# Activation blocks of a Strassen-Winograd down projection: summed by spreading and adding DMAs in DRAM instead of by GpSimd in SBUF

## The chip, the cores and the metric

The kernel runs on one NeuronCore of a Trainium2 chip. TensorE (PE) multiplies into PSUM; PEld is its weight load. VectorE (DVE) and ScalarE (ACT) do the elementwise work, GpSimd (POOL) does a little of it and issues its own DMAs, and SyncE (SP) issues the other DMAs. Each engine takes its instructions in order, and semaphores tie the engines together. The metric is the device time of one execution in microseconds (us), the median over repeated runs.

## The reference

One decoder layer on x of 1024 positions by 1024 channels, float32: RMSNorm, a joint input projection for a retention group (4 heads) and a gated spatial group (4 groups), an output projection with a residual, then the part that matters here, and a last RMSNorm:

```python
h = rmsnorm(x, ffn_norm_g[l])
up = causal_depthwise_conv(h @ w_up[l], conv_w[l], conv_b[l])   # width 3
a, bgate = jnp.split(up, [D_FF], axis=-1)                       # D_FF = 2816
x = x + (jax.nn.silu(a) * bgate) @ w_down[l]
```

## The kernel before, in words

Channels lie on the 128 partitions and positions on the free axis, so 2816 channels are 22 tiles of 128 x 1024. All matmuls work on float32 split into a high and a low part (`split_w`, L113 and L114: a ScalarE copy `h` and a VectorE difference `l`), and each of the three big projections is cut into 2 x 2 blocks and done with seven block products instead of eight.

**Up projection and gate.** `unit` (u3 to u21) makes the two 128 x 1024 rows `ra` and `rb` of one channel tile: PE sums products in PSUM banks (X, Y, Z, L147), ScalarE and VectorE take them out (L205, L221, L228, L247, L160), and both prepare the next unit's weights. `conv` (L791, L800, L803) then works on a finished pair: ScalarE scales `ra` into a tile `cv` (L788), VectorE adds two shifted taps (L791), ScalarE applies silu (L800), and `gate` multiplies by the other branch (L803). Tiles `cv`, `ra` and `rb`, and many others, are drawn from one ring of 38 buffers (`up`); a new tile's first writer waits until the last reader of the old one is through.

**Activation blocks.** Tiles 2j and 2j+1 (called `e` and `o`, pair j, 11 pairs) are the upper and lower row block of the down projection's activation, and the halves 0 and 1 of the positions are its column blocks. `blocks_of` (L814 to L822) makes the seven blocks that the seven products need and stores them in the DRAM tile `gb`, in four DMAs from GpSimd's queue; four of the blocks are differences, made by four GpSimd subtractions per pair (L820) in place.

**Down projection.** The seven products run in the order `SEQ` = 2, 1, 5, 6, 3, 7, 4. `load_act` (L851) fetches a product's blocks, two pairs at a time, and splits them (L852, L853); product 2's fetches (g20 to g24) go through GpSimd's queue, the rest through SP's. `load_wt` (L868) fetches the weights. `down` (L893) multiplies and `acc` (L898) adds a PSUM result to the residual rows `x2`. For the last pair, products 2 and 1 take their block from SBUF directly.

PE's order is written out by hand from u20 on; everything else, on every engine, is ordered by a planner that simulates the program. Names in traces drop their numbers: `cv` is any gate tile, `gb` the DRAM blocks.

Of the kernel before, what the change touches and what calls it, by code (L numbers as in the profile page):

```python
# [10 lines left out]
F32 = mybir.dt.float32  # L11
F32R = mybir.dt.float32r
AF = mybir.ActivationFunctionType
ALU = mybir.AluOpType

P = 128
# [8 lines left out]
HALF = 512  # L25
# [40 lines left out]
def decoder_layer(ctx, tc, io, out):  # L66
    nc = tc.nc
# [8 lines left out]
    def U(name, dt=F32, shape=(P, 1024)):  # L76
        return up.tile(list(shape), dt, tag="u", name=name)
# [4 lines left out]
    def A(name):  # L82
        return pp.tile([P, HALF], F32, tag="acc", name=name, bufs=5)

    def M(name, shape=(P, 512)):
        return pp.tile(list(shape), F32, tag="sm", name=name, bufs=3)
# [16 lines left out]
    hs = lambda t, h: t[:, h * HALF:(h + 1) * HALF]  # L103
# [18 lines left out]
    def split(src, name):  # L122
        h, l = U(name + "h", F32R, src.shape), U(name + "l", F32R, src.shape)
        nc.scalar.activation(h, src, AF.Copy)
        nc.vector.tensor_tensor(l, src, h.bitcast(F32), ALU.subtract)
        return h, l
# [25 lines left out]
    class Unit:  # L152
# [9 lines left out]
        def prep(u, src, key, eng=None):  # L162
            h, l = split_w(src, u.name + key, eng=eng)
            return [(h[:, o:o + u.kh], l[:, o:o + u.kh]) for o in range(0, src.shape[1], u.kh)]
# [293 lines left out]
    for half in range(2):  # L458
        ps = M(f"r1bc{half}")
# [14 lines left out]
    def small4(name, f, n=4):  # L474
        ps = M(name, (P, 4, P))
        for j in range(n):
            f(ps[:, j], j)
        return ps
# [15 lines left out]
    for h in range(NH):  # L494
# [10 lines left out]
        for half in range(2):  # L505
            ps = small4(f"pS{h}{half}", lambda o, j: nc.tensor.matmul(o, kT[:, cut(half * 4 + j)], qT[:, cut(half * 4 + j)], start=True, stop=True))
# [189 lines left out]
    for u in us:  # L696
        h, l = split(u.wa, u.name + "a")
# [77 lines left out]

    BLK = {k: i for i, k in enumerate(("R11", "R21", "R22", "T1", "T3", "T4", "T2"))}
    gbs = [dp.tile([P, 7, n, HALF], F32, name=f"gb{n}") for n in (KH - 1, 1)]
    halves = lambda t: t.rearrange("p (a b) -> p a b", b=HALF)  # L780

# [17 lines left out]
    def silu(t):  # L799
        nc.scalar.activation(t, t, AF.Silu)  # L800

    def gate(i, a, b, eng=None):
        (eng or nc.vector).tensor_tensor(a, a, b, ALU.mult)  # L803
        g[i] = halves(a)

    g = {}
# [1 line left out]
    def conv(ra, rb, i):  # L808
        a = Taps(ra, i).all()
        silu(a)  # L810
        gate(i, a, Taps(rb, FT + i).all())


    def blocks_of(j):  # L814
        e, o = g.pop(2 * j), g.pop(2 * j + 1)
        gb, j = gbs[j // (KH - 1)], j % (KH - 1)
        nc.gpsimd.dma_start(gb[:, 0, j], e[:, 0])  # L817
        nc.gpsimd.dma_start(gb[:, 1:3, j], o)  # L818
        for x, y, z in ((e[:, 0], e[:, 1], e[:, 0]), (e[:, 1], o[:, 1], e[:, 1]), (o[:, 1], o[:, 1], e[:, 0]), (o[:, 0], o[:, 0], o[:, 1])):
            nc.gpsimd.tensor_tensor(x, y, z, ALU.subtract)  # L820
        nc.gpsimd.dma_start(gb[:, 3:5, j], e)
        nc.gpsimd.dma_start(gb[:, 5:7, j], o)  # L822

    class Up(Unit):
        def __init__(u, i):
# [16 lines left out]
    def load_act(i, j):  # L842
        n = min(2, KH - 2 * j)
        src = gbs[0][:, BLK[KEY[i]], 2 * j:2 * j + 2] if n == 2 else gbs[1][:, BLK[KEY[i]]]
        if n == 2:
            h, l = [U(f"g{i}{j}{x}", F32R, PAIR) for x in "hl"]
        else:
            e = U(f"g{i}{j}e", F32R, PAIR)
            h, l = e[:, :1], e[:, 1:]
        x = l.bitcast(F32)  # L850
        (nc.gpsimd if i == SEQ[0] else nc.sync).dma_start(x, src)  # L851
        nc.scalar.activation(h, x, AF.Copy)  # L852
        nc.vector.tensor_tensor(l, x, h.bitcast(F32), ALU.subtract)  # L853
        act[i] += [(h[:, m], l[:, m]) for m in range(n)]

    def last_act(i, x):
# [27 lines left out]
    def load_x2(n):  # L884
        x2[n] = U(f"x2{n}")
        nc.sync.dma_start(x2[n], x2d[:, n])

    def down(ps, i, p, start, ks, stop, cols=slice(0, HALF)):
        first = start
        todo = [(k, s) for k in ks for s in range(2)] + [(k, 2) for k in ks]  # L890
        for n, (k, s) in enumerate(todo):
            w, r = wts[i][p * KH + k], act[i][k]
            nc.tensor.matmul(ps, w[s // 2], r[s % 2][:, cols], start=first, stop=stop and n == len(todo) - 1, skip_group_check=True)  # L893
            first = False

    def acc(n, half, ps):
        o = hs(x2[n], half)
        nc.vector.tensor_tensor(o, ps, o, ALU.add)  # L898

    PREP = {2: [(load_act, j) for j in range(5)]}  # L900
    for i in SEQ[1:]:
        PREP[i] = [(f, int(j)) for f, j in zip([load_act, load_act, load_wt] * 3 + [load_wt] * 3, "010231452345")]
        if i == 1:
            PREP[i] = [(load_act, j) for j in range(5)] + [(load_wt, j) for j in range(6)]
# [10 lines left out]
    def conv_next():  # L915
        nonlocal done
        conv(*todo[done], done)
        if done % 2:
            blocks_of(done // 2)
        done += 1  # L920
# [36 lines left out]
    e, o = g[FT - 2], g[FT - 1]  # L957
    last_act(2, o[:, 0])
    last1 = U("g1e", F32R, PAIR)
    nc.scalar.activation(last1[:, 0], e[:, 0], AF.Copy)  # L960
    nc.vector.tensor_tensor(last1[:, 1], e[:, 0], last1[:, 0].bitcast(F32), ALU.subtract)
    blocks_of(KH - 1)


# [24 lines left out]
    Z = [M(f"dZ{p}") for p in range(3)] + [A("dZ3")]  # L989
# [3 lines left out]
    for p in range(4):  # L993
        down(Z[p], 2, p, False, [KH - 1], True)
        if p:
            load_x2(2 * p + 2) if p < 3 else None
        acc(2 * p, 0, Z[p])
    prep(1, 20)
    act[1].append((last1[:, 0], last1[:, 1]))
    for i, nxt in zip(SEQ[1:-1], SEQ[2:]):  # L1000
        for p in range(4):
            prep(nxt, 3)
            if i in (1, 6, 7):
                if i == 1:
                    X[p] = A(f"dX{p}")
                ps = X[p]
            else:
                if i == 5:
                    load_x2(2 * p + 1)
                ps = M(f"dY{i}{p}")  # L1010
            down(ps, i, p, i in (1, 5, 3), range(KH), True)
            for n, half in {1: [(0, 0)], 5: [(0, 1), (1, 1)], 6: [(0, 1)], 3: [(0, 1)], 7: [(1, 1)]}[i]:
                acc(2 * p + n, half, ps)
            if i == 7:
                for b in (ba, bb, bc):
                    b.square(2 * p)
    manual.close()

    with tc.manual_schedule(engines={mybir.EngineType.PE, mybir.EngineType.DVE, mybir.EngineType.Activation}):
# [8 lines left out]
        for k in range(8):  # L1028
            s, p = divmod(k, 4)
            b = (bb, bc)[s]  # L1030
            ps = X[p][:, b.blk]
            down(ps, 4, p, False, range(KH), True, b.blk)
            y = x2[2 * p + 1][:, b.blk]
# [51 lines left out]
```

## Time and profile before

| | us |
|---|---|
| median of 3 runs | 1063.68 |
| lowest, highest | 1059.34, 1066.58 |
| profiled execution, its own time | 1061.0 |
| its span | 1059.2 |
| PE busy in the span | 1023.9 (97%) |
| DVE busy | 823.0 (78%) |
| ACT busy | 486.6 (46%) |
| POOL busy | 173.3 (16%) |
| mean granted TensorE clock | 0.993 of full |

Times in the trace are microseconds from the span's start. The up projection with its gates fills about 440 to 833, the down projection 833 to the end. A row of a group of instructions gives line, engine, operation, output and inputs, shapes and count, then busy time, mean duration in ns, and the idle time of that engine just before, with what ended it. A row of the timeline gives start, duration, engine, line, what was done, and in brackets the idle time before it and its releaser.

### The profile page before, as it was taken

The numbers are of one execution on the slowest core, as the hardware profiler recorded it, in microseconds if no ns is written. First come the engines' busy times: TensorE is split into PE (matmuls) and PEld (weight loads), VectorE is DVE, ScalarE is ACT, GpSimd is POOL, SyncE is SP. The second block draws the span as 40 slices with busy tenths as digits, with TensorE's granted clock in tenths as the row PEclk, the third lists the DMA queues.
The fourth block names the chain that finished last, engine by engine and source line by source line (L and its number), as shares of the span: only waits on it lengthen the run. The fifth ranks groups of instructions, "written<-read, shape, count | busy, mean of one in ns | idle before, by whom it ended". The sixth has DMA issues, their size and how long they took to land.

```text
span 1059.2 us, 12678 instructions
## 1 busy us (share of the span) xinstructions
PE 1023.9 (97%) x4794; PEld 846.7 (80%) x4794; DVE 823.0 (78%) x1022; ACT 486.6 (46%) x684; POOL 173.3 (16%) x132
## 2 busy tenths in 40 slices
PE   7899999999999999999999999999999999999996
PEld 5677888888888888788888778778888888878896
DVE  6958886968968378856789998987869877886565
ACT  6563444334364253535445535444535643344440
POOL 0002330411310000000214152323034120000000
PEclk9989999999999999999999999999999999999998
DMA  8151031121356240011323233332244788974514
GB/s 301 68 199 40 23 110 63 49 81 62 99 197 222 100 159 20 21 60 58 113 90 114 106 129 129 110 119 99 82 149 132 263 308 295 372 242 151 203 51 159
DMA packets 48445, 141.57 MB, mean 134 GB/s; under 512 B 5056, under 2 KB 9536, under 8 KB 48384
## 3 DMA queue, kind: packets, MB, share of 16 engines
q1 hardware_dynamic: 42032, 117.96, 32.3%
q0 software_dynamic: 6352, 22.81, 5.7%
q8 instruction: 37, 0.61, 0.2%
q14 instruction: 24, 0.20, 0.1%
HBM read 109.03 MB, written 31.72 MB: 133 GB/s over the span
## 4 chain that ended last, share of the span: by engine, by line
PE 72%; DVE 17%; issue 5%; ACT 4%; DMA 1%; POOL 1%; SPq 0%; DVEq 0%; ACTq 0%; POOLq 0%
PE dX L893 11%; PE po L135 8%; PE dY L893 6%; DVE cv L791 3%; PE dZ L893 3%; PE G3X L147 1%; PE G1X L147 1%; PE A3X L147 1%; PE B3X L147 1%; PE u2X L147 1%; PE u21X L147 1%; PE u20X L147 1%; PE u18X L147 1%; PE u3X L147 1%; PE A0X L147 1%
## 5 line engine op out<-in xcount | busy, mean ns | idle before, releaser
L817 POOL DMA_DIRECT2D gb<-cv x11 | 6.5, 588 | 265.3 <-DVE cv L803 254.3
L800 ACT ACTIVATE cv<-cv 128x1024 f32<-128x1024 f32 x22 | 23.3, 1059 | 47.7 <-DVE cv L791 47.7
L820 POOL TENSOR_TENSOR cv<-cv 128x512 f32<-128x512 f32 x22 | 40.1, 1825 | 26.3 <-DMA gb<-cv 14.9
L820 POOL TENSOR_TENSOR cv<-cv,cv 128x512 f32<-128x512 f32 x22 | 36.4, 1656 | 4.9 <-DMA gb<-cv 2.8
L818 POOL DMA_DIRECT2D gb<-cv x11 | 7.8, 710 | 127.7 <-DVE cv L803 127.7
L803 DVE TENSOR_TENSOR cv<-cv,cv 128x1024 f32<-128x1024 f32 x22 | 26.8, 1218 | 0.0
L650 DVE TENSOR_TENSOR xr<-po,xr 128x512 f32<-128x512 f32 x16 | 10.8, 688 | 19.9 <-PE po L135 19.9
L973 ACT ACTIVATE x3q<-x 128x256 f32<-128x256 f32 (+1 forms) x21 | 9.3, 483 | 33.1 <-DVE x L1034 28.2
L656 ACT ACTIVATE xq<-xr 128x512 f32<-128x512 f32 x14 | 8.8, 628 | 24.1 <-DVE xr L650 17.0
L541 ACT ACTIVATE sT<-po 128x128 f32<-128x128 f32 x32 | 8.4, 277 | 13.3 <-PE po L533 13.2
L878 DVE TENSOR_TENSOR wd<-wd,wd 128x1024 f32<-128x1024 f32 (+1 forms) x6 | 6.8, 1135 | 9.4 <-DMA wd<-in_w_down 9.4
L975 DVE TENSOR_TENSOR sq<-sq,x3q 128x256 f32<-128x256 f32 (+1 forms) x20 | 9.8, 516 | 4.2 <-ACT x3q L973 3.8
L984 DVE SCALAR_TENSOR_TENSOR x<-x,vec,r 128x256 f32<-128x256 f32 (+1 forms) x24 | 12.0, 566 | 0.8 <-PE r L617 0.8
L660 DVE TENSOR_TENSOR sq<-sq,xq 128x512 f32<-128x512 f32 x13 | 8.9, 688 | 3.2 <-ACT xq L656 3.0
L875 DVE TENSOR_TENSOR ds<-wd,wd 128x1024 f32<-128x1024 f32 (+1 forms) x6 | 6.8, 1134 | 5.8 <-DMA wd<-in_w_down 5.8
L341 DVE SCALAR_TENSOR_TENSOR x<-x,vec,x 128x512 f32<-128x512 f32 x16 | 11.0, 747 | 0.0
L670 ACT ACTIVATE nx<-xr,vec 128x512 f32<-128x512 f32 x16 | 10.8, 708 | 0.0
L504 ACT ACTIVATE kn<-pk,vec 128x512 f32<-128x512 f32 x8 | 5.2, 680 | 11.8 <-PE pk L503 11.8
L360 ACT ACTIVATE xn<-xn 128x1024 f32<-128x1024 f32 x8 | 8.4, 1053 | 3.4 <-DMA xn<-in_xN 3.2
L673 DVE TENSOR_TENSOR nx<-nx,r 128x1024 f32<-128x1024 f32 x8 | 9.5, 1216 | 0.4 <-PE r L617 0.4
L1034 DVE TENSOR_TENSOR x<-dX,x 128x256 f32<-128x256 f32 x8 | 3.4, 424 | 8.0 <-PE dX L893 8.0
L898 DVE TENSOR_TENSOR x<-dY,x 128x512 f32<-128x512 f32 x12 | 8.1, 685 | 1.4 <-DMA x<-x2d 1.4
(5664 smaller groups left out, 3795.7 us busy)
## 6 DMA issues: line engine op xcount, KB each, us to landing
wd<-in_w_down SPq DMA_DIRECT2D x45, 512.0 KB, 4.4
gb<-cv POOLq DMA_DIRECT2D x33, 512.0 KB, 3.3
wo<-in_w_out SPq DMA_DIRECT2D x10, 512.0 KB, 3.7
x<-in_xT SPq DMA_DIRECT2D x8, 512.0 KB, 9.2
xn<-in_xN SPq DMA_DIRECT2D x8, 512.0 KB, 6.7
xr<-in_xT SPq DMA_DIRECT2D x8, 512.0 KB, 6.0
x2d<-xr SPq DMA_DIRECT2D x8, 512.0 KB, 3.1
x<-x2d SPq DMA_DIRECT2D x8, 512.0 KB, 7.2
```

The lines of the kernel that those rows point to most:

```text
L135: nc.tensor.matmul(ps, a, b, start=(k == 0 and t == 0), stop=(k == n - 1 and t == 2))
L147: nc.tensor.matmul(ps, a[:, k], b, start=(start and i == 0), stop=(i == 3 * n - 1), skip_group_check=not start)
L341: nc.vector.scalar_tensor_tensor(o[:, m], x[:, m], V("g1", 2 * j + m), y[:, m], ALU.mult, op)
L650: nc.vector.tensor_tensor(u.y, u.ps, u.y, ALU.add)
L670: nc.scalar.activation(nx[n // 2][:, n % 2], xr[th][n // 2][:, n % 2], AF.Identity, scale=V("g2", n))
L791: nc.vector.scalar_tensor_tensor(u.t[:, d:], u.r[:, :S - d], V("cw", 88 - 44 * d + u.i), u.t[:, d:], ALU.mult, ALU.add)
L800: nc.scalar.activation(t, t, AF.Silu)
L803: (eng or nc.vector).tensor_tensor(a, a, b, ALU.mult)
L820: nc.gpsimd.tensor_tensor(x, y, z, ALU.subtract)
L893: nc.tensor.matmul(ps, w[s // 2], r[s % 2][:, cols], start=first, stop=stop and n == len(todo) - 1, skip_group_check=True)
L975: nc.vector.tensor_tensor(sq[:, u.blk], sq[:, u.blk], u.t, ALU.add)
L984: nc.vector.scalar_tensor_tensor(y, y, V("gf", n), u.nr.rs, ALU.mult, ALU.mult)
```

## The change

`blocks_of` no longer subtracts. `gate` multiplies each half of the positions by itself, and one of the halves (half 1 of an even tile, half 0 of an odd one) comes out negated, by a scalar_tensor_tensor with -1. With the signs set, every block is a sum of halves, and the blocks are laid out in `gb` so that each half goes to neighbouring ones: three DMAs per pair write a half into 4, 2 and 1 blocks at once (one source, repeated), then three DMAs with `accum_op=add` add a half to 4, 2 and 1 blocks that are already there. The three adding DMAs of a pair overlap one another's blocks, so each waits for the one before. Products 2 and 5 get negated blocks, and `acc` subtracts their results; product 4's block is negated back while it is split.

```diff
-    BLK = {k: i for i, k in enumerate(("R11", "R21", "R22", "T1", "T3", "T4", "T2"))}
+    BLK = {k: i for i, k in enumerate(("R11", "T1", "T4", "T2", "T3", "R22", "R21"))}
...
-    def gate(i, a, b, eng=None):
-        (eng or nc.vector).tensor_tensor(a, a, b, ALU.mult)
+    def gate(i, a, b):
+        neg = 1 - i % 2
+        for k in range(2):
+            o, x = hs(a, k), hs(b, k)
+            if k == neg:
+                nc.vector.scalar_tensor_tensor(o, o, -1.0, x, ALU.mult, ALU.mult)
+            else:
+                nc.vector.tensor_tensor(o, o, x, ALU.mult)
         g[i] = halves(a)
...
     def blocks_of(j):
         e, o = g.pop(2 * j), g.pop(2 * j + 1)
         gb, j = gbs[j // (KH - 1)], j % (KH - 1)
-        nc.gpsimd.dma_start(gb[:, 0, j], e[:, 0])
-        nc.gpsimd.dma_start(gb[:, 1:3, j], o)
-        for x, y, z in ((e[:, 0], e[:, 1], e[:, 0]), (e[:, 1], o[:, 1], e[:, 1]), (o[:, 1], o[:, 1], e[:, 0]), (o[:, 0], o[:, 0], o[:, 1])):
-            nc.gpsimd.tensor_tensor(x, y, z, ALU.subtract)
-        nc.gpsimd.dma_start(gb[:, 3:5, j], e)
-        nc.gpsimd.dma_start(gb[:, 5:7, j], o)
+        def put(blk, x, **kw):
+            n = blk[1] - blk[0]
+            nc.gpsimd.dma_start(gb[:, blk[0]:blk[1], j], x.unsqueeze(1).to_broadcast([P, n, HALF]), **kw)
+
+        put((0, 4), e[:, 0])
+        put((4, 6), o[:, 1])
+        put((6, 7), o[:, 0])
+        put((1, 5), e[:, 1], accum_op=ALU.add)
+        put((2, 4), o[:, 1], accum_op=ALU.add)
+        put((2, 3), o[:, 0], accum_op=ALU.add)
...
-        nc.scalar.activation(h, x, AF.Copy)
-        nc.vector.tensor_tensor(l, x, h.bitcast(F32), ALU.subtract)
+        if i == 4:
+            nc.scalar.activation(h, x, AF.Copy, scale=-1.0)
+            nc.vector.scalar_tensor_tensor(l, x, -1.0, h.bitcast(F32), ALU.mult, ALU.subtract)
+        else:
+            nc.scalar.activation(h, x, AF.Copy)
+            nc.vector.tensor_tensor(l, x, h.bitcast(F32), ALU.subtract)
...
-    def acc(n, half, ps):
+    def acc(n, half, ps, op=ALU.add):
         o = hs(x2[n], half)
-        nc.vector.tensor_tensor(o, ps, o, ALU.add)
+        nc.vector.tensor_tensor(o, o, ps, op)
...
-        acc(2 * p, 0, Z[p])
+        acc(2 * p, 0, Z[p], ALU.subtract)
...
-                acc(2 * p + n, half, ps)
+                acc(2 * p + n, half, ps, ALU.subtract if i == 5 else ALU.add)
```

The planner's order moves with it. On GpSimd's queue, pair 0 (its tiles are cv_3739 for `e`, cv_3874 or cv_3875 for `o`) stands before so, the waits in brackets (DMASW is a semaphore of GpSimd's DMAs):

```order
L817 DMA gb_3525<-cv_3739 128x512 [waits DVE_49]
L820 TENSOR_TENSOR cv_3739<-cv_3739 128x512 [waits DMASW0_49,DMAHW7_49,PE_49,Activation_49]
L818 DMA gb_3525<-cv_3874 128x2x512 [waits DVE_49]
L820 TENSOR_TENSOR cv_3739<-cv_3874,cv_3739 128x512 [waits Pool_49]
L821 DMA gb_3525<-cv_3739 128x2x512 [waits Pool_49]
L820 TENSOR_TENSOR cv_3874<-cv_3874,cv_3739 128x512 [waits DMAHW1_49,DMASW1_49,DMAHW2_49,PE_49,Activation_49]
L820 TENSOR_TENSOR cv_3874<-cv_3874 128x512 [waits Pool_49]
L822 DMA gb_3525<-cv_3874 128x2x512 [waits Pool_49]
```

and in the changed kernel so, with the three plain DMAs first and the three adding ones behind them:

```order
L827 DMA gb_3525<-cv_3739 128x4x512 [waits DVE_49,Activation_49]
L827 DMA gb_3525<-cv_3875 128x512 [waits DVE_49,Activation_49]
L827 DMA gb_3525<-cv_3875 128x2x512 [waits DVE_49]
L827 DMA gb_3525<-cv_3739 128x4x512 [waits DMASW2_49,DMASW0_49]
L827 DMA gb_3525<-cv_3875 128x2x512 [waits DMASW3_49]
L827 DMA gb_3525<-cv_3875 128x512 [waits DMASW4_49]
```

The four subtractions are gone; the last three DMAs each wait for DMAs of the same pair to land.

On ACT, the buffer of pair 1's `e` goes to another tile. Before, the first `cv` of u5 waited for DVE and ACT alone:

```order
L205 ACTIVATE u8p_4344<-u8X 128x512 [waits PE_49]
L113 ACTIVATE u8ch<-u8t 128x1024 [waits PE_49]
L788 ACTIVATE cv_4305<-u5ra,vec 128x1024 [waits DVE_49,Activation_49]
L788 ACTIVATE cv_4310<-u5rb,vec 128x1024 [waits DVE_49]
L113 ACTIVATE u8dh<-u8w_4324 128x512 [waits DMAHW7_49,PE_49,Activation_49]
L221 ACTIVATE u8p_4381<-u8Y 128x512 [waits PE_49]
```

and in the changed kernel:

```order
L205 ACTIVATE u8p_4344<-u8X 128x512 [waits PE_49]
L789 ACTIVATE cv_4306<-u5ra,vec 128x1024 [waits DMASW6_49,DMASW1_49]
L789 ACTIVATE cv_4311<-u5rb,vec 128x1024 [waits DVE_49,Activation_49]
L113 ACTIVATE u8dh<-u8w_4324 128x512 [waits DMAHW7_49,PE_49]
L221 ACTIVATE u8p_4381<-u8Y 128x512 [waits PE_49]
L228 ACTIVATE u8p_4395<-u8X 128x512
```

The `cv` tile of u5 now waits for both DMAs that read pair 1's `e`, the 4-block write and the 4-block add; u8's weight split and its PSUM copies stand behind it.

At the end of the up projection GpSimd's queue also carries the fetches of product 2 (g20 to g24). Before:

```order
L851 DMA g22l<-gb_3525 128x1024 [waits PE_49]
L818 DMA gb_3525<-cv_6001 128x2x512 [waits DVE_49]
L820 TENSOR_TENSOR cv_5866<-cv_6001,cv_5866 128x512 [waits Pool_49]
L821 DMA gb_3525<-cv_5866 128x2x512 [waits Pool_49]
L820 TENSOR_TENSOR cv_6001<-cv_6001,cv_5866 128x512 [waits DMASW0_49,Activation_49]
L851 DMA g23l<-gb_3525 128x1024 [waits DMASW2_49,Activation_49]
L820 TENSOR_TENSOR cv_6001<-cv_6001 128x512 [waits Pool_49]
L822 DMA gb_3525<-cv_6001 128x2x512 [waits DMASW3_49,Pool_49]
L851 DMA g24l<-gb_3525 128x1024 [waits DMAHW5_49,DMAHW2_49,PE_49]
```

and in the changed kernel:

```order
L827 DMA gb_3525<-cv_6002 128x512 [waits DMASW1_49,DVE_49,Activation_49]
L863 DMA g22l<-gb_3525 128x1024 [waits PE_49]
L827 DMA gb_3525<-cv_6002 128x2x512 [waits DVE_49]
L827 DMA gb_3525<-cv_5866 128x4x512 [waits DMASW6_49,DMASW3_49]
L863 DMA g23l<-gb_3525 128x1024 [waits DMASW5_49,Activation_49]
L827 DMA gb_3525<-cv_6002 128x2x512 [waits DMASW4_49]
L863 DMA g24l<-gb_3525 128x1024 [waits DMAHW2_49,DMASW7_49,DMAHW5_49,DMASW1_49,PE_49]
L827 DMA gb_3525<-cv_6002 128x512 [waits DMASW6_49,DMASW0_49]
```

g23 now stands behind an adding DMA's wait for pair 9's writes, and g24 behind another one's wait for that adding DMA.

## Rows read from the trace of the kernel before

**Rows 1.** windows: length, busy by engine (instructions), clock, DMA share, GB/s.

```profile
600.00:700.00 100.00, 96.27 (x421) 78.38 (x420) 92.22 (x91) 50.81 (x62) 34.50 (x28) 1.00 0.33 116
...
850.00:900.00 50.00, 50.00 (x222) 41.44 (x221) 35.92 (x37) 19.68 (x21) 6.78 (x7) 1.00 0.81 299
```

**Rows 2.** PE's waits, 490 to 865: total us, times, longest us.

```profile
PE u14Y L147 <- ACT u14p L221: 1.8, 1, 1.8
PE u9Y L147 <- ACT u9p L221: 1.6, 1, 1.6
PE u11Y L147 <- ACT u11bh L113: 1.0, 1, 1.0
PE u15Y L147 <- ACT u15p L221: 0.9, 1, 0.9
PE u13X L147 <- DVE u13rb L160: 0.8, 1, 0.8
PE u6Y L147 <- ACT u6p L221: 0.5, 1, 0.5
```

**Rows 3.** timeline, 583 to 588: DVE and ACT.

```profile
584.08 2.31 DVE L791 SCALAR_TENSOR_TENSOR cv<-u6ra,vec,cv 128x1022 f32<-128x1022 f32 x1
...
587.45 1.27 DVE L791 SCALAR_TENSOR_TENSOR cv<-u6rb,vec,cv 128x1022 f32<-128x1022 f32 x1
...
586.48 1.06 ACT L800 ACTIVATE cv<-cv 128x1024 f32<-128x1024 f32 x1 [6.31 <-DVE cv L791]
```

**Rows 4.** page, costliest groups: subtractions, gate, other VectorE forms.

```profile
L820 POOL TENSOR_TENSOR cv<-cv,cv 128x512 f32<-128x512 f32 x22 | 36.4, 1656 | 4.9 <-DMA gb<-cv 2.8
...
L803 DVE TENSOR_TENSOR cv<-cv,cv 128x1024 f32<-128x1024 f32 x22 | 26.8, 1218 | 0.0
...
L341 DVE SCALAR_TENSOR_TENSOR x<-x,vec,x 128x512 f32<-128x512 f32 x16 | 11.0, 747 | 0.0
...
L898 DVE TENSOR_TENSOR x<-dY,x 128x512 f32<-128x512 f32 x12 | 8.1, 685 | 1.4 <-DMA x<-x2d 1.4
```

**Rows 5.** timeline, DVE: first and last instruction stretched beside POOL.

```profile
538.98 1.46 DVE L114 TENSOR_TENSOR u7bl<-u7s,u7bh 128x1024 fp32r<-128x1024 f32 x1
...
862.36 2.67 DVE L114 TENSOR_TENSOR wd11l<-wd,wd11h 128x1024 fp32r<-128x1024 f32 x1
```

**Rows 6.** DMA issues: KB of each, median us to landing.

```profile
gb<-cv POOLq DMA_DIRECT2D x33, 512.0 KB, 3.3
...
gb<-cv POOLq DMA_DIRECT2D x11, 256.0 KB, 2.5
...
x<-in_xT SPq DMA_DIRECT2D x8, 512.0 KB, 9.2
```

**Rows 7.** timeline of pairs 0 and 1: gates, buffer reusers, PE.

```profile
512.75 1.22 DVE L803 TENSOR_TENSOR cv<-cv,cv 128x1024 f32<-128x1024 f32 x1
...
526.37 1.24 ACT L788 ACTIVATE cv<-u2rb,vec 128x1024 f32<-128x1024 f32 x1 [3.50 <-DMA gb<-cv]
...
551.64 1.22 DVE L803 TENSOR_TENSOR cv<-cv,cv 128x1024 f32<-128x1024 f32 x1
...
563.90 1.25 ACT L788 ACTIVATE cv<-u5rb,vec 128x1024 f32<-128x1024 f32 x1 [2.25 <-DVE cv L803]
...
565.57 0.58 ACT L221 ACTIVATE u8p<-u8Y 128x512 f32<-128x512 f32 x1
...
568.32 0.39 PE L147 MATMUL u8Y<-R220h,u8ch 128*128 128x512 f32 x1
```

**Rows 8.** timeline of the stage's end: tile 19's gate, g24, PE.

```profile
810.57 1.22 DVE L803 TENSOR_TENSOR cv<-cv,cv 128x1024 f32<-128x1024 f32 x1
...
823.15 0.57 POOL L851 DMA_DIRECT2D g24l<-gb  x1
...
832.11 1.22 DVE L853 TENSOR_TENSOR g24l<-g24l,g24h 128x1024 fp32r<-128x1024 f32 x1 [0.22 <-ACT g24h L852]
...
836.62 0.39 PE L893 MATMUL dZ<-g24h,wd21h 128*128 128x512 f32 x1
```

## The prediction

> **What bounds the kernel now.** I read the windows of the whole core first, to find where PE is not busy, then PE's own waits there, then the timeline of the instructions ahead of each wait, and last the DMA issues. The windows say that PE is the bound nearly everywhere: 50.0 of 50 us in the down projection's first stretch, 96.3 of 100 in the middle of the up projection, where VectorE is busy for 92.2 of the 100 [rows 1]. So the most this change can win is what PE loses in the stage of the gates. Four waits of PE there, 1.8, 1.6, 1.0 and 0.9 us, are 5.3 us; two of 0.8 and 0.5 [rows 2] and one of 0.2 bring it to 6.8 us. The first four are for ScalarE, but ScalarE is only passing on a delay: before u9's wait it sat idle 6.3 us until VectorE finished a tap, and stood with PE's PSUM copy behind that silu [rows 3].
>
> That tap took 2.31 us; the same form took 1.27 us three us later, when GpSimd had no subtraction running [rows 3]. This is the second thing to see: GpSimd's subtractions and VectorE's two-input instructions slow each other. The subtractions with two inputs from both tiles average 1.66 us [rows 4]. From 490 to 865 there are 29 stretched VectorE instructions, first and last in [rows 5]; each less its undisturbed duration, they sum to 27.8 us.
>
> **The change, part by part.**
>
> *Subtractions removed.* All 44 go, and with them VectorE's 27.8 us. The stage is not VectorE-bound throughout, so that isn't 27.8 us of time: it is worth PE's waits that stand behind stretched instructions. Ahead of u9's wait the two taps lost 1.0 us each against a wait of 1.6 [rows 2, 3]; ahead of the other three the timeline shows stretched instructions worth more than the wait too. I take all four: -5.3 us, bounds 0 and -6.8.
>
> *Gate split.* One instruction of 1.218 us becomes a scalar_tensor_tensor of half the width, 0.747, and a tensor_tensor of half the width, 0.685 [rows 4]: +0.21 us, 22 times, +4.7 us of VectorE. It is spread over 370 us in which VectorE gets 27.8 us back, so it costs PE nothing; without that cover it would lengthen the waits by about 0.2 us each.
>
> *acc and product 4.* `acc` only swaps operands and the operation. Product 4's split changes from a tensor_tensor to a scalar_tensor_tensor of 1024, +0.06 us by the halves of [rows 4], six times, beside matmuls: nothing.
>
> *Adding DMAs.* This operation is not in the trace. Plain stores of these blocks take 2.5 us for 256 KB and 3.3 us for 512 KB, so 1.7 us and 0.8 us per block [rows 6]. An adding DMA must fetch what it adds to, so it cannot be below the plain price, which for 4 blocks is 4.9 us. The other end is the slowest 512 KB row, 9.2 us when all queues start at once [rows 6], twice for 1 MB: 18.4 us. I take the size part twice (a read and a write of each destination byte), since these stores meet a half-idle DMA: 8.1 us for 4 blocks, 4.9 for 2, 3.3 for 1. Nearest are the plain rows, from the same queue and buffers.
>
> From the end of the gate of `o`, the 4-block add lands after two issues (0.6 us each, as [rows 8] shows one), a plain 512 KB store and the add: 1.2 + 3.3 + 8.1 = 12.6 us; bounds 9.4 and 22.9. The other two follow one by one: 12.6 + 4.9 + 3.3 = 20.8 us; bounds 15.2 and 36.7.
>
> *Who waits for that.* The ring of buffers hands `e` and `o` on, and the new writer waits in order on ScalarE or VectorE.
> - Pair 0's gate ends at 513.97, so its add lands at 526.6. ScalarE already waited for such a store there, until 526.37 [rows 7]. The tile that now waits has one `cv` instruction less behind it ahead of PE's copies: 0.
> - Pair 1's gate ends at 552.86, the add lands at 565.5. Behind the waiting `cv` stand the second `cv`, u8's weight split and the copy of u8Y, which ended at 566.15 and which PE wanted at 568.32 [rows 7]. Now: 565.5 + 1.15 for the `cv`, then 2.25 us as from 563.90 to 566.15, so 568.9: PE waits 0.6 us. With the lower bound nothing, with the upper (575.8) 10.9 us.
> - The end of the stage: the gate of tile 19 ends at 811.8; the 4-block add is issued 4.5 us later and lands at 824.4, only then g24 can be issued, 1.8 us later than the 823.15 of before counting the issue in between. Before, its split ended at 833.3 and PE used it at 836.62 [rows 8], 3.3 us to spare: 0. With the upper bound (834.7 and then 2 blocks of traffic ahead) about 12 us.
> - Later pairs have longer between the gate and the reuse than these two; I give them 0, and a share in the upper case.
>
> *DMA traffic.* Seven block writes per pair become seven writes and seven adds. By 0.8 us a block, twice, that is 11 us of DMA time per pair: harmless in the stage (DMA share 0.33), but the last pair's falls into a stretch with share 0.81 [rows 1]. The first down products lose no PE time now; bounds 0 and +5; I take +1.
>
> *Sum.* -5.3 + 0.6 + 1.0 = -3.7 us, on the profiled execution's own 1061.0 us (span 1059.2): 1057.3. That execution lies 2.7 us under the median of the three runs, 1063.7, so on the median it is **1060.0 us**, 0.35% less.
>
> The Trainium skill, "DMA: Bandwidth & Descriptors", section "Rules for kernel authors", speaks against the change: an accumulating DMA reads its destination and writes it later, so a later access of the same bytes has to wait for the earlier DMA's semaphore. By that rule the chain of three adds is serial, and the added waits in the changed order agree; no run so far shows their length. The same page, section "Anatomy of one DMA", fits a DMA of this queue as about 2.0 us plus its bytes at 436 GB/s and prices no addition: by that estimate 1 MB takes 4.4 us, pair 1's wait goes away, and the sum would be -4.3 us, 1059.4.
>
> **The rivals.**
> 1. *Forecast* (chance 0.62): VectorE's relief shows in PE's waits, the adds stay under their cover: 1054 to 1066 on the median.
> 2. *The idle only moves* (0.16). PE's order is drawn anew for the units from u6 on, and ScalarE's queue with it; a new wait takes the place of the four. For it: ScalarE's copies stand behind silu and taps in the changed order as well. Against: 23 us less VectorE work net. Relief 0 to 2, plus the two costs: 1062 to 1067, unchanged.
> 3. *The adds are slow* (0.17), the other side. If the 4-block add takes more than about 12 us, buffer reuse and g24 decide. Each further us costs 1 at pair 0, 1 at pair 1, and 2 at the end (g24 stands behind two adds); pairs 2 to 4 join near the end of the range. At 12 us the stalls are some 4 + 4 + 6 = 14, the net +9 with the relief, 1073; at the upper bound of 18.4 they are 11 + 11 + 12, and perhaps 10 for the later pairs, net +39: 1103. For it: nothing in the trace adds in DRAM. Against: the plain rows leave twice their price free.
> 4. *More than is visible is won* (0.05). Only if fewer stretched instructions also shorten the end of the stage, beyond PE's 6.8 us: 1050 to 1053.
>
> **How the numbers follow.** About 1%, 10.6 us, is what a measurement of this kernel can tell from no change. Faster by over 1% needs a time under 1053.0: rival 4 alone, and not all of it: 0.04. Slower by over 1% is over 1074.3: nearly all of rival 3: 0.16. The rest, 0.80, is within 1%. The range goes from 1053 (the whole of PE's 6.8 us, and the scatter of the three runs, 1059.3 to 1066.6, about the median) to 1076, which takes in rival 2 and the mild end of rival 3; left out are about 0.14 above and 0.04 below. The forecast's own range is 1054 to 1066.
>
> **What would show it.** In the profile after: VectorE's taps and splits all at their undisturbed durations (1.28 and 1.22), VectorE's busy time down by some 23 us, POOL's by 76; the waits of u9, u11, u14 and u15 gone; adds of 4 blocks landing in 5 to 12 us; `cv` of u2 and u5 waiting for `gb` on ScalarE by 2 to 6 us; g24 split before about 836. Wrong would be: adds of 4 blocks over 12 us, ScalarE or VectorE waiting for `gb` by 10 us or more with PE behind them, or new PE waits of 5 us between 500 and 833.

## The result: 1.4% slower

| us | before | changed |
|---|---|---|
| median, 5 runs each on one chip | 1063.36 | 1077.54 |
| lowest, highest | 1059.34, 1066.58 | 1075.77, 1079.15 |
| ratio, 95% interval | | 1.014, 1.0123 to 1.0157 |
| profiled execution, its span | 1059.2 | 1074.3 |
| DVE busy, POOL busy | 823.0, 173.3 | 797.8, 126.7 |
| PE busy for the same 4794 matmuls | 1023.9 | 1028.1 |
| mean granted TensorE clock | 0.993 | 0.986 |

The forecast was 1060.0 us in a range of 1053 to 1076. The time lies above the range, and the change costs 14.2 us where 3.7 were to be won.

**The profile after.** PE's waits between 490 and 960 us, in total us, times, and longest:

```profile
PE dX L909 <- DVE g64l L869: 3.5, 1, 3.5
PE u6Y L147 <- ACT u6p L221: 2.8, 1, 2.8
PE u8Y L147 <- ACT u8p L221: 2.5, 1, 2.5
PE dZ L909 <- ACT g24h L868: 2.5, 1, 2.5
PE dY L909 <- DVE x L914: 2.5, 1, 2.5
PE u10Y L147 <- ACT u10p L221: 1.5, 1, 1.5
PE u10X L147 <- ACT u10p L205: 0.8, 1, 0.8
PE dZ L909 <- DVE g24l L869: 0.8, 1, 0.8
PE u8X L147 <- ACT u8p L205: 0.4, 1, 0.4
```

The waits of u9, u11, u14 and u15 [rows 2] are gone, as forecast, but longer ones stand in their place: at the first pairs (u6, u8, u10), at the end of the stage (g24), and in the first down products (x, g64). Windows of the changed kernel, columns as in [rows 1]:

```profile
530.00:535.00 5.00, 5.00 (x12) 3.94 (x13) 5.00 (x7) 3.45 (x4) 0.90 (x1) 0.50 0.58 90
575.00:580.00 5.00, 5.00 (x24) 4.13 (x23) 5.00 (x7) 3.06 (x4) 0.86 (x1) 1.00 1.04 283
600.00:700.00 100.00, 97.68 (x430) 80.23 (x429) 83.65 (x97) 51.89 (x62) 18.67 (x21) 1.00 0.70 180
840.00:845.00 5.00, 4.27 (x10) 3.41 (x11) 4.88 (x6) 3.62 (x5) 0.00 (x0) 0.50 0.99 312
850.00:900.00 50.00, 50.00 (x222) 41.42 (x221) 34.91 (x38) 20.82 (x22) 5.45 (x6) 1.00 0.95 307
900.00:960.00 60.00, 54.03 (x222) 43.39 (x221) 47.48 (x49) 21.34 (x23) 0.00 (x0) 0.94 0.81 290
```

The last three columns are granted clock, DMA share and GB/s. DMA share went from 0.33 to 0.70 in the stage of the gates and from 0.81 to 0.95 in 850 to 900 [rows 1]. And PE, once it has stood for 2.8 us at u6, runs 530 to 535 at 0.50, that is 1.2 GHz: all 5 us busy, yet 12 matmuls and not 22, so a further 2.3 us is lost. The same follows the wait for g24 (10 matmuls in 840 to 845). In 900 to 960, where PE waits for x and g64, the clock was 0.94 on average, and 1.00 in the kernel before. It did not fall behind u8's wait of 2.5 us (575 to 580 at 1.00).

The rows of the gate's two halves answer to the gate in [rows 4]; the DMA issues answer to [rows 6], plain and adding ones mixed:

```profile
L809 DVE SCALAR_TENSOR_TENSOR cv<-cv,cv 128x512 f32<-128x512 f32 x22 | 15.2, 689 | 0.0
L811 DVE TENSOR_TENSOR cv<-cv,cv 128x512 f32<-128x512 f32 x22 | 15.1, 688 | 0.0
...
gb<-cv POOLq DMA_DIRECT2D x22, 1024.0 KB, 8.6
gb<-cv POOLq DMA_DIRECT2D x22, 512.0 KB, 5.6
```

How one add becomes a wait of PE is read off pair 0. The first fence has the end of the gate on VectorE and GpSimd's timeline, the second ScalarE and PE. They answer to [rows 7]:

```profile
510.83 0.69 DVE L811 TENSOR_TENSOR cv<-cv,cv 128x512 f32<-128x512 f32 x1
...
511.84 1.28 POOL L827 DMA_DIRECT2D gb<-cv  x2 [22.18 <-DVE cv L811]
517.01 1.36 POOL L827 DMA_DIRECT2D gb<-cv  x1 [3.88 <-DMA gb<-cv]
527.32 1.18 POOL L827 DMA_DIRECT2D gb<-cv  x1 [8.95 <-DMA gb<-cv]
533.24 0.90 POOL L827 DMA_DIRECT2D gb<-cv  x1 [4.74 <-DMA gb<-cv]
```

```profile
527.11 1.24 ACT L789 ACTIVATE cv<-u2ra,vec 128x1024 f32<-128x1024 f32 x1 [8.00 <-DMA gb<-cv]
...
529.25 0.58 ACT L221 ACTIVATE u6p<-u6Y 128x512 f32<-128x512 f32 x1
...
529.89 0.80 PE L147 MATMUL u6Y<-R220h,u6ch 128*128 128x512 f32 x1 [2.81 <-ACT u6p L221]
...
570.96 1.24 ACT L789 ACTIVATE cv<-u5ra,vec 128x1024 f32<-128x1024 f32 x1 [7.61 <-DMA gb<-cv]
```

The 4-block add is issued at 517.01, once the plain stores have landed; the next issue, which waits for it, comes 10.3 us later. ScalarE's `cv` of u2, which takes over pair 0's buffer, stands 8.00 us for the same landing; the copy `u6p` is queued behind it, and PE stands behind that. The `cv` of u5 stands 7.61 us for pair 1's add in the same way. At the end of the stage (GpSimd, against [rows 8]) product 2's fetches stand among pair 9's adds:

```profile
812.99 0.73 POOL L827 DMA_DIRECT2D gb<-cv  x1
821.25 1.34 POOL L827 DMA_DIRECT2D gb<-cv  x1 [7.53 <-DMA gb<-cv]
822.07 1.09 POOL L863 DMA_DIRECT2D g23l<-gb  x1
831.30 1.19 POOL L827 DMA_DIRECT2D gb<-cv  x1 [8.14 <-DMA gb<-cv]
832.03 1.05 POOL L863 DMA_DIRECT2D g24l<-gb  x1
```

g24's fetch is issued at 832.03, not 823.15.

### The profile page after: what moved, and what is told of

Read it like the earlier page. It is cut to its first block, busy times and chain, and to the rows that moved or that the text cites. A ratio compares the mean times of both kernels' runs of the same rounds, so it can differ in the third digit from the quotient of the medians.

```text
span 1074.3 us, 12691 instructions
## 1 busy us (share of the span) xinstructions
PE 1028.1 (96%) x4794; PEld 850.3 (79%) x4794; DVE 797.8 (74%) x1044; ACT 487.0 (45%) x684; POOL 126.7 (12%) x110
## 3 DMA queue, kind: packets, MB, share of 16 engines
q0 software_dynamic: 16560, 43.00, 17.3%
## 5 line engine op out<-in xcount | busy, mean ns | idle before, releaser
L827 POOL DMA_DIRECT2D gb<-cv x66 | 60.6, 961 | 510.0 <-DVE cv L809 199.1
L650 DVE TENSOR_TENSOR xr<-po,xr 128x512 f32<-128x512 f32 x16 | 10.9, 689 | 19.9 <-PE po L135 18.7
L809 DVE SCALAR_TENSOR_TENSOR cv<-cv,cv 128x512 f32<-128x512 f32 x22 | 15.2, 689 | 0.0
L811 DVE TENSOR_TENSOR cv<-cv,cv 128x512 f32<-128x512 f32 x22 | 15.1, 688 | 0.0
L360 ACT ACTIVATE xn<-xn 128x1024 f32<-128x1024 f32 x8 | 8.4, 1053 | 3.0 <-DMA xn<-in_xN 2.8
L914 DVE TENSOR_TENSOR x<-x,dY 128x512 f32<-128x512 f32 x12 | 8.1, 682 | 2.0 <-DMA x<-x2d 2.0
L792 DVE SCALAR_TENSOR_TENSOR cv<-u2ra,vec,cv 128x1023 f32<-128x1023 f32 (+1 forms) x2 | 2.6, 1279 | 8.0 <-ACT cv L789 8.0
L891 DVE TENSOR_TENSOR ds<-ds,wd 128x1024 f32<-128x1024 f32 (+1 forms) x6 | 6.8, 1136 | 1.9 <-DMA wd<-in_w_down 1.7
L914 DVE TENSOR_TENSOR x<-x,dX 128x512 f32<-128x512 f32 x12 | 8.2, 682 | 0.0
```

The lines of the kernel that those rows point to most:

```text
L650: nc.vector.tensor_tensor(u.y, u.ps, u.y, ALU.add)
L809: nc.vector.scalar_tensor_tensor(o, o, -1.0, x, ALU.mult, ALU.mult)
L811: nc.vector.tensor_tensor(o, o, x, ALU.mult)
L827: nc.gpsimd.dma_start(gb[:, blk[0]:blk[1], j], x.unsqueeze(1).to_broadcast([P, n, HALF]), **kw)
L914: nc.vector.tensor_tensor(o, o, ps, op)
```

## The experiments

The theory (A): the time goes to work that waits for the length of the adds, at three places (first pairs' buffers, g24, last pair). The main rival (B): the redrawn order of work, the split gates or the number of chained DMAs do it, whatever the DMAs compute. Each ratio is to the kernel before on the same chip (medians 1062.0 to 1062.7 us, 1063.4 beside the changed kernel); differences between two altered kernels, which were not timed side by side, are of medians, and uncertain by some 1 to 2 us.

**1. The adding alone (e1_plain).**

```diff
-        put((1, 5), e[:, 1], accum_op=ALU.add)
-        put((2, 4), o[:, 1], accum_op=ALU.add)
-        put((2, 3), o[:, 0], accum_op=ALU.add)
+        put((1, 5), e[:, 1])
+        put((2, 4), o[:, 1])
+        put((2, 3), o[:, 0])
```

> The changed kernel with its three adding DMAs of a pair turned into plain stores of the same blocks, in the same order with the same waits; the sums of the blocks are left out. Theory A (the adding itself is long: 4 blocks took 9.8 to 12.0 us from its issue to that of the DMA chained behind it, and buffers, g24 and the down projection's fetches stand behind it): a plain 4-block store takes about 5 us, u6, u8 and u10 wait under 1 us, the split of g24 comes about 8 us earlier, and the time falls to 1056 to 1066 us. Rival B (the number of chained DMAs, their waits on one another, or the order of work drawn anew): the 11 pairs still chain, PE still waits over 1.5 us at u6, u8 and u10, and the time stays at 1073 to 1078 us.

1059.17 us, ratio 0.997 (0.9955 to 0.9985): 18.4 us under the changed kernel. The blocks then hold no sums. Every engine's instructions and waits stand in the same order as in the changed kernel, so this difference is the adding and nothing else. Rival B falls: with the same order and the same chain of DMAs the time is below that of the kernel before. GpSimd's timeline of pair 0, and PE's waits:

```profile
519.75 0.78 POOL L827 DMA_DIRECT2D gb<-cv  x1 [3.58 <-DMA gb<-cv]
525.45 0.71 POOL L827 DMA_DIRECT2D gb<-cv  x1 [4.92 <-DMA gb<-cv]
528.87 0.58 POOL L827 DMA_DIRECT2D gb<-cv  x1 [2.71 <-DMA gb<-cv]
```

```profile
PE dX L909 <- DVE g64l L869: 3.5, 1, 3.5
PE dY L909 <- DVE x L914: 2.5, 1, 2.5
PE u8X L147 <- ACT u8p L205: 0.4, 1, 0.4
```

From issue to the issue behind it, the 4-block DMA takes 5.7 us plain and 10.3 adding (8.4 to 12.0 over the 11 pairs), the 2-block one 3.4 and 5.9. The waits of u6, u8Y, u10 and g24 are gone; those of x and g64 are unchanged, so they do not come from the adding.

**2. The relief alone (e4_nosub).** The kernel before without its four subtractions:

```diff
-        for x, y, z in ((e[:, 0], e[:, 1], e[:, 0]), (e[:, 1], o[:, 1], e[:, 1]), (o[:, 1], o[:, 1], e[:, 0]), (o[:, 0], o[:, 0], o[:, 1])):
-            nc.gpsimd.tensor_tensor(x, y, z, ALU.subtract)
```

> The kernel before with GpSimd's four subtractions per pair left out (the blocks then hold the halves as they are), all else as before: what the relief of VectorE is worth alone. Theory A (prediction's first term: PE's waits at u9, u11, u14 and u15 go, 5.3 us, at most 6.8): 1056 to 1059 us, 4.5 to 7 us under the kernel before. Rival B (the relief only moves idle time, as PE's order is drawn by the planner): less than 2 us under it.

1053.24 us, ratio 0.992 (0.9895 to 0.9945): 9.4 us under the kernel before, more than either theory said. Not all else is as before: the planner drew a new order on every engine (on PE, 181 of 4794 matmuls stand at another place), so the 9.4 us are the relief together with that order; experiment 7 bears on the two. Its window shows how the size was to be seen:

```profile
600.00:700.00 100.00, 100.00 (x443) 82.78 (x442) 86.46 (x96) 53.55 (x65) 9.55 (x14) 1.00 0.34 119
```

A PE that never waits does 443 matmuls in 100 us, 0.226 us each. The kernel before did 421 there [rows 1]: 22 fewer, 5.0 us, though its busy column lacks only 3.7. A matmul's row lasts 0.39 us and the next starts 0.226 us after it, so each wait shows about 0.16 us too short, and short ones not at all. The same count over 500 to 850, of this kernel, the kernel before, the changed one and experiment 1:

```profile
500.00:850.00 350.00, 350.00 (x1546) 289.79 (x1545) 285.51 (x307) 183.73 (x218) 30.76 (x47) 1.00 0.39 136
```

```profile
500.00:850.00 350.00, 342.94 (x1503) 281.00 (x1502) 303.66 (x300) 177.73 (x212) 100.37 (x84) 1.00 0.37 127
```

```profile
500.00:850.00 350.00, 338.68 (x1462) 277.57 (x1461) 270.44 (x310) 172.40 (x207) 56.94 (x64) 0.98 0.67 174
```

```profile
500.00:850.00 350.00, 349.62 (x1543) 289.00 (x1542) 285.21 (x326) 183.80 (x218) 44.96 (x67) 1.00 0.52 185
```

The kernel before has 43 matmuls fewer than a PE that never waits, 9.7 us, against the 9.4 measured. The changed kernel has 84 fewer, 19.0 us, and experiment 1, with the adding taken out, 3.

**3. Gate split and redrawn order (e12_split).** The kernel of experiment 2 with the changed kernel's `gate`:

```diff
-    def gate(i, a, b, eng=None):
-        (eng or nc.vector).tensor_tensor(a, a, b, ALU.mult)
+    def gate(i, a, b):
+        neg = 1 - i % 2
+        for k in range(2):
...
```

> The kernel before with the subtractions left out and the gate's product cut in two halves, one of them negated, as the changed kernel has it; the seven plain stores a pair stay, the blocks hold the halves as they are. The order of work is drawn anew with the two half gates. Theory A (split and new order are covered by VectorE's idle time): within 2 us of the kernel without subtractions, 1051 to 1056 us. Rival B (the new order, and not the adding, makes new waits of PE): 1058 us or more, with waits of over 1.5 us between 500 and 840.

1054.04 us, ratio 0.9911 (0.9885 to 0.9938), 0.8 us above experiment 2 with ranges that overlap (1051.70 to 1056.22, and 1052.49 to 1056.63). PE does not wait between 500 and 850. The split costs nothing that can be measured. The order tests little here: it is nearly that of experiment 2 (14 of PE's 4794 matmuls at another place, none of ScalarE's instructions) and not that of the changed kernel, which experiment 1 has. Experiment 1 writes 14 blocks a pair plainly where this kernel writes 7, and its order is another: the two together cost 5.1 us.

**4. The first pairs (e7_first).** Pairs 0 to 2 of the changed kernel by GpSimd, the rest by adding DMAs:

```diff
+        if pair in (0, 1, 2):
+            put((0, 1), e[:, 0])
+            put((5, 6), o[:, 1])
+            put((6, 7), o[:, 0])
+            for x, y, z in ((e[:, 0], e[:, 0], e[:, 1]), (e[:, 1], o[:, 1], e[:, 1]), (o[:, 1], o[:, 1], e[:, 0]), (o[:, 0], o[:, 0], o[:, 1])):
+                nc.gpsimd.tensor_tensor(x, y, z, ALU.add)
+            nc.gpsimd.dma_start(gb[:, 1:5:3, j], e)
+            nc.gpsimd.dma_start(gb[:, 2:4, j], o)
+            return
```

> The changed kernel with pairs 0, 1 and 2 alone built by GpSimd's additions and plain stores. Theory A (the buffers of these pairs are held until a 4-block add of some 10 us has landed, and PE loses 2.3 to 2.8 us each at u6, u8 and u10, with some 3 us of low clock): these waits go, up to 1 us comes back for VectorE's instructions stretched beside GpSimd's additions, and the time falls by 7 to 10 us, to 1068 to 1071 us. Rival B (the changed order of ScalarE's queue makes those waits): they stay, the time falls by less than 3 us.

1066.61 us, ratio 1.0044 (1.0029 to 1.006): 10.9 us under the changed kernel, 1.4 under the expected range. u6, u8 and u10 no longer wait; u9's 1.6 us beside GpSimd's arithmetic is back. PE's and ScalarE's orders move here too, but experiment 1 lost the same waits in the changed kernel's own order. The waits at g24, x and g64 stay:

```profile
PE dX L919 <- DVE g64l L879: 3.5, 1, 3.5
PE dZ L919 <- ACT g24h L878: 2.4, 1, 2.4
PE dY L919 <- DVE x L924: 1.7, 1, 1.7
PE u9Y L147 <- ACT u9p L221: 1.6, 1, 1.6
PE dZ L919 <- DVE g24l L879: 0.8, 1, 0.8
```

**5. Product 2's fetches (e3_sp).**

```diff
-        (nc.gpsimd if i == SEQ[0] else nc.sync).dma_start(x, src)
+        nc.sync.dma_start(x, src)
```

> The changed kernel with the fetches of product 2 (g20 to g24) issued from SP's queue and not from GpSimd's, so that none of them stands in program order behind an adding DMA's wait. Theory A (g24 is late because its issue stands behind two adding DMAs of pair 9 on GpSimd's queue): g24h's matmul no longer waits 2.5 us at the start of product 2's last part, the clock there stays up, and the time falls by 4 to 7 us, to 1070 to 1074 us. Rival B (the gate of pair 9 or the DMA's own queue sets it; or SP's queue, which carries 8 weight loads at that place, now holds weight fetches behind g23 and g24): the wait of 2.5 us stays or moves to a weight tile, and the time is within 2 us of the changed kernel's or above it.

1068.94 us, ratio 1.0068 (1.0044 to 1.0092): 8.6 us under the changed kernel, more than A expected. The waits for g24 and x are gone and g64's is 1.7 us; those at u6, u8 and u10 stay. The planner's order moves on every engine but PE here, from 798 us on, so the run shows that g24 need not be late, and not that its queue is worth all of the 8.6. Up to there every instruction stands as in the changed kernel, and yet u6 waits 4.6 us and not 2.8: by so much one execution's waits can differ.

**6. The last pair (e2_last).** Experiment 4's branch for pair 10 alone (`if pair == 10`).

> The changed kernel with the last pair's blocks alone (pair 10) built by GpSimd's additions in SBUF and plain stores, 7 blocks written and none added in DRAM. Theory A (in the first down products PE lost some 8.6 us because the last pair's adds fill the DMA queues: x2d landed 2.0 us late, g64l 3.5 us, and the clock fell after both): these two waits go, DMA share in 850 to 900 falls from 0.95 to about 0.8, and the time falls by 6 to 9 us against the changed kernel, to 1068 to 1072 us. Rival B (those transfers are late because all of the stage runs late, or because the chained DMAs of pair 9 are): it falls by less than 3 us.

1072.2 us, ratio 1.0098 (1.0067 to 1.0129): 5.3 us under the changed kernel, a little less than A's 6 to 9. The waits for x and g64 are gone, and the DMA share falls from 0.95 to 0.83:

```profile
850.00:900.00 50.00, 50.00 (x222) 41.39 (x222) 41.78 (x42) 25.70 (x27) 9.01 (x9) 1.00 0.83 305
```

It is about the size of the 5.1 us between experiments 3 and 1, which speaks for twice the written blocks, in a stretch where the DMA engines are busy for 0.95 of the time. It is not shown apart: experiment 5 ends the wait for x and half of g64's with the last pair's DMAs as they were, at a DMA share of 1.00 in the same stretch.

**7. All three at once (e8_mix).** GpSimd's additions for pairs 0, 1, 2 and 10, the fetches on SP's queue, adding DMAs for pairs 3 to 9.

> The changed kernel with all three costly places taken out: pairs 0, 1, 2 and 10 built by GpSimd's additions, product 2's fetches on SP's queue, adding DMAs for pairs 3 to 9 only. Theory A (the costs are these three places and add up: -8.6 us for the queue, -5.3 us for the last pair, and 7 to 10 us for the first pairs): 1053 to 1058 us, about 0.5% or more under the kernel before. Rival B (the costs overlap, one wait standing in for the next): 1060 to 1066 us, no better than the kernel before.

1054.07 us, ratio 0.9932 (0.9907 to 0.9957): 8 us under the kernel before, and 23.5 under the changed one, against 10.9 + 8.6 + 5.3 = 24.8 for the three apart. The costs add up; rival B falls. Of the kernels here that leave nothing out this is the fastest, within 1 us of experiment 2, which sums nothing. All that PE waits for between 490 and 960:

```profile
PE dX L919 <- DVE g65e L879: 2.3, 1, 2.3
PE u9Y L147 <- ACT u9p L221: 1.6, 1, 1.6
```

It also bears on experiment 2. PE's order here is that of the kernel before but for 14 of 4794 places, ScalarE's but for 8 of 687. Before 600 us, where GpSimd adds for pairs 0 to 2, PE loses 10 matmuls to a PE that never waits, and the kernel before lost 11; from 600 to 800, without GpSimd's arithmetic, it loses none, and the kernel before lost 32. That speaks for the arithmetic, and not the order, as what cost PE its time.

**8. One pair fewer on GpSimd (e10_mix3).** As 7, with `if pair in (0, 1, 10)`.

> The mixed kernel (product 2's fetches on SP's queue, the last pair by GpSimd's additions) with pair 2 built by adding DMAs again, so that GpSimd adds for pairs 0, 1 and 10 alone. Theory A (pair 2's buffer is wanted before its 4-block add has landed: u10 waited 1.5 and 0.8 us for it in the changed kernel; against it u9's wait of 1.6 us beside GpSimd's additions goes): within 2 us of the mixed kernel, 1052 to 1057 us. Rival B (the cost of the first pairs is a chain that any of them starts): 1058 us or more.

1056.39 us, ratio 0.9944 (0.9923 to 0.9965). The order is that of 7 on every engine but GpSimd. u10 waits 1.5 and 1.0 us again, u6 0.6, and u9 does not. It stands 2.3 us above 7, where 2 were allowed, with intervals that overlap: pair 2 can go to either side.

**9. The same adds, cut to free `e` early (e9_early, e11_early_mix).**

```diff
         put((0, 4), e[:, 0])
-        put((4, 6), o[:, 1])
+        put((4, 5), e[:, 1])
+        put((1, 4), e[:, 1], accum_op=ALU.add)
+        put((5, 6), o[:, 1])
         put((6, 7), o[:, 0])
-        put((1, 5), e[:, 1], accum_op=ALU.add)
-        put((2, 4), o[:, 1], accum_op=ALU.add)
+        put((2, 5), o[:, 1], accum_op=ALU.add)
         put((2, 3), o[:, 0], accum_op=ALU.add)
```

> The changed kernel with the same number of added blocks (7 a pair) cut otherwise: the e tile is written to block 4 plainly and added to blocks 1 to 3 as soon as it is there, and the o tile then added to blocks 2 to 4 in one DMA and to block 2 in another. The e buffer is so freed without o's gate, and behind o's gate stand two adds (3 blocks, 1 block) and not three (4, 2, 1). Theory A (what costs time is what waits for the adds, at the first pairs' buffers and at g24, not their number of bytes): u6, u8 and u10 wait under 1 us, g24 comes earlier, and the time falls by 8 to 14 us against the changed kernel, to 1063 to 1069 us; x2d and g64l are still late. Rival B (the bytes read and written by the adds load the DMA queues everywhere): it stays within 4 us of the changed kernel.

> The early cut of the adds (e to block 4 plainly and added to 1 to 3, then o added to 2 to 4 and to 2) for pairs 0 to 9, the last pair by GpSimd's additions, product 2's fetches on SP's queue. Theory A: no wait of PE over 1 us between 490 and 900 us, x2d and g64l nearly in time, 1053 to 1059 us. Rival B (bytes of the adds): 1064 us or more.

1069.08 us (ratio 1.0065, 1.004 to 1.0091) and 1063.28 us (1.001, 0.9991 to 1.0029). The first lies 0.1 us above its range and 8.5 under the changed kernel, so its rival B, the bytes of the adds, falls. The second misses A's range and does not reach B's. In e9_early g24 is in time on GpSimd's queue, as two adds for three should give; in e11_early_mix it goes by SP's queue anyhow. But u6 still waits, 3.0 and 5.1 us, where under 1 was expected, and u7 now 1.3 and 2.7. ScalarE's two rows in e9_early, and then GpSimd's last add of pair 0, say why:

```profile
520.34 1.23 ACT L789 ACTIVATE cv<-u2ra,vec 128x1024 f32<-128x1024 f32 x1
...
527.86 1.24 ACT L789 ACTIVATE cv<-u2rb,vec 128x1024 f32<-128x1024 f32 x1 [5.82 <-DMA gb<-cv]
```

```profile
523.67 0.93 POOL L827 DMA_DIRECT2D gb<-cv  x1 [6.70 <-DMA gb<-cv]
```

`e` is indeed free early: u2's first `cv` no longer waits for a DMA. Its second takes the buffer of pair 0's `o`, and `o` is read by two chained adds. The last of them could be issued only at 523.67, when the one before it had landed, and the `cv` starts at 527.86, upon its landing. So the new cut moved the wait from `e` to `o`: whichever tile the chain of adds reads last is held longest.

## Why the prediction was wrong

Experiments 2, 3 and 1 are steps on the way from the kernel before to the changed one, and split the 14.9 us between 1062.65 and 1077.54: -9.4 (subtractions out, with the order drawn for it), +0.8 (gate split), +5.1 (14 written blocks a pair, with the changed kernel's order), +18.4 (seven of them adding). Against the prediction's own terms, which other experiments price:

| step | predicted | measured | by |
|---|---|---|---|
| subtractions removed | -5.3 | -9.4 | e4_nosub |
| gate split | 0 | within noise (+0.8) | e12_split |
| first pairs wait for the adds | +0.6 | +10.9 | e7_first |
| g24 behind pair 9's adds | 0 | up to +8.6 | e3_sp |
| DMA traffic, last pair | +1.0 | +5.3 | e2_last |

- **Relief.** The mechanism was right and the size too small; even its bound of -6.8 fell short. VectorE's own gain was sized well: its busy time fell by 25.2 us beside the 3.5 that the split gates add, so 28.7 against 27.8. PE's share of it was summed over listed waits, where a count of matmuls by window, begun in [rows 1] with 421 in 100 us, would have given 9.7.
- **Gate split at nothing** held. The half-width scalar_tensor_tensor took 0.689 us, not the 0.747 of the row taken for it [rows 4].
- **The add's price.** 8.1 us was taken for 4 blocks; it took 10.1 us from its issue to the landing that ScalarE saw (517.01 to 527.11). Doubling the size part was right: by experiment 1 a block more costs 1.1 us plain and 2.2 adding. The plain price was too low, 0.8 us a block. The Trainium skill's fit ("DMA: Bandwidth & Descriptors", section "Anatomy of one DMA"), by which the prediction estimated 4.4 us, is too low even for the plain store, 5.7 to the next issue. By the Trainium skill's section "Rules for kernel authors" on the same page, an add has to wait for the semaphore of an earlier DMA of the same bytes; the trace agrees, 10.3 and 5.9 us from issue to issue.
- **"Pair 0: 0" is the step that failed first.** From the end of the gate to the landing 12.6 us were forecast. From 511.52, where the gate ended, to 527.11 it was 15.6: 0.3 to the stores' issue, 5.2 from there to the add's issue at 517.01 (4.5 were taken for both), and 10.1 for the add and not 8.1. No cover was left there: before, the landing came 12.4 us behind the gate (513.97 to 526.37) and already ended in a wait of PE of 0.5 us [rows 2, 7]. So 3.2 us came on top, less 1.0 for a silu that no longer stands between the waiting `cv` and the copy `u6p` (the rows of before are below). That makes 2.7 us, and PE waited 2.8. At pair 1, which was given 0.6 us, PE waited 2.5, and at pair 2, which was given 0, 1.5 and 0.8.

```profile
528.51 1.05 ACT L800 ACTIVATE cv<-cv 128x1024 f32<-128x1024 f32 x1
529.47 0.58 ACT L221 ACTIVATE u6p<-u6Y 128x512 f32<-128x512 f32 x1
```

- **Rival 3 was the right mechanism with the wrong point.** It asked for adds over 12 us. Adds of 10 were enough, as only the add's own length was judged and not that of the stores ahead of it: at g24, forecast at 0 with 3.3 us to spare, the plain store ahead took 8.3 us to the add's issue (812.99 to 821.25) at a DMA share of 0.84 in 800 to 850, not 3.3, and the add 10.
- **A term that was missing: the clock.** The sum counted waits alone. After the longer ones PE ran at 1.2 GHz for some microseconds, which cost 2.3 us in 530 to 535 alone.
- **The signs.** None of the signs that the prediction named for being wrong came: no 4-block add over 12.0 us, no wait of ScalarE for `gb` of 10 us (8.0 and 7.6), no wait of PE of 5 us. Several waits of 2 to 3.5 us were enough.
- **Rival 2 (new order)** is refuted by experiment 1: in the changed kernel's very order PE loses 3 matmuls, 0.7 us, between 500 and 850. What the order may cost in the down projection lies within the 5.1 us.

What stays open: how much of e3_sp's 8.6 us is the queue and how much the order drawn with it, how much of the 5.1 and 5.3 us at the last pair is the written blocks, and why u8's 2.5 us wait left the clock up.

## What to carry to other kernels

An adding DMA into DRAM relieves the engines but holds its source buffer and its queue nearly twice as long as a plain store (10.3 us against 5.7 here): use it where the buffer is not soon reused, where nothing urgent is queued behind it, and where the DMA engines have room (pairs 3 to 9 here), and leave the other pieces where they were; here that split won 0.7% and the wholesale change lost 1.4%. A chain of adds holds the tile that it reads last the longest, so check every tile of the chain and not the first alone. Where a wait already ends at the critical engine, price a longer one in full. Weigh a relief by counting the bound engine's instructions per window against a stretch that never waits, not by its listed waits.

## What the runs showed of the hardware

The same 43.00 MB of GpSimd's DMAs make 11632 packets and 11.0% of the 16 engines' time as plain stores, 16560 packets and 17.3% with the adds. The page's DMA queue rows, of e1_plain and then of the changed kernel:

```profile
q0 software_dynamic: 11632, 43.00, 11.0%
```

```profile
q0 software_dynamic: 16560, 43.00, 17.3%
```

GpSimd's own issue is longer as well: 1.36 us for a 4-block add, 0.78 for the plain store of the same blocks. Its 66 issues of block DMAs take 60.6 us where the 44 of before took 30.0, so its busy time fell by 46.6 us and not by the 76 that the prediction named.
